# A block's products with the values issued after the next block's scores, modulation's transposes as a step of their own, and three plain pairs in the gated feed-forward

## Chip, cores, metric

One core of a Trainium2 chip. The metric is the device time of one execution in microseconds (us), smaller is better; the time of a kernel is the median of its runs.

## What is computed

Two layers of a diffusion-transformer block over 1024 latent tokens and, in layer 0, 256 context tokens beside them (1280 in all), width 1024, all in float32. Cut to what matters here:

```python
for layer in range(DEPTH):                                    # DEPTH = 2
    mod = silu(c) @ w_ada[layer] + b_ada[layer]               # modulation: shifts, scales, gates
    u = modulate(rmsnorm(x, g), sh1, sc1) @ w_in[layer]       # in-projection
    gla = gla_output(gla_chunked(q, k, v, g_fwd) + flip(gla_chunked(flip(q, k, v, g_bwd))), r)
    x = x + g1 * (concat([gla, short_conv, neighbourhood_attention]) @ w_out[layer])
    h = modulate(rmsnorm(x, norm_ffn_g[layer]), sh2, sc2)
    x = x + g2 * conv_ffn(h, w_up, conv_w, conv_b, w_down)    # dwconv3(h @ w_up), silu(a) * b, @ w_down

# gla_chunked, chunks of 16 tokens, decays b = cumsum(g):
a = where(causal, einsum(q * exp(b), k * exp(-b)), 0)         # scores inside a chunk
o = einsum(a, v) + einsum(q * exp(b), s)                      # values, and the carried state
s = s * exp(b_last) + einsum(k * exp(b_last - b), v)
```

## The kernel before, in words

Every product of the large projections is made of three TensorE matmuls on halves of the float32 numbers (`mm3`, L146 to L148: high by high, low by high, high by low). A layer runs in stages: modulation and norm, the in-projection, the gated linear attention (GLA), the neighbourhood attention (NA), `w_out`, then the feed-forward's up and down products. A scheduler sets one order for each engine when the program is built, and each engine then runs its list strictly in that order. The profile's names: PE is TensorE, DVE VectorE, ACT ScalarE, POOL GpSimd, SP the queue that issues most DMAs.

**GLA.** `gla_pair` is called for three pairs of heads. Its first loop goes over five blocks of 256 tokens: decayed keys, two transposes (L549), a copy by ACT (L551), the state products (L555). A scan by DVE (L571) then carries the state over all chunks. Its second loop goes over the output blocks, five in layer 0 and four in layer 1, so 27 in all. One block is: POOL copies the states it needs to `g_sw` (L585, L588); DVE builds the decayed queries `zq` in four operations (L601), the keys `g_k`, the masked decays `g_m` (L611) and `g_qd` (L614); PE makes the scores (L627, L635, L642) in PSUM; DVE copies the causal part to `zd` (L645), ACT copies the rest to `g_at` (L650), and DVE and POOL add into `g_at` (L653); then PE multiplies the state (L658) and the values (L662) into one PSUM bank; ACT takes the result and its square (L667, L669), PE averages the squares (L672), a gating chain follows and a DMA stores the block (L684). `zq`, `g_k` and `g_sw` have one buffer each.

PE has little of its own to do there. So `fill(cols)` draws dense in-projection matmuls from a list of generators: 1024 columns' worth after the state loop's steps, 1536 (`FO`) ahead of the scores, ahead of the values and ahead of the averages. `gla_gates` prepares the next pair's decays, also between the blocks (its products are L495). `run_background(1)`, once for each token block of the dense products, runs one step of the next layer's or stage's modulation: `ada_steps` (L158 to L194) makes four 256-column products (L176) and an addition by DVE (L181) in each of eight steps, and in the eighth, right behind that addition, two transposes by PE (L185) and the additions that store them (L189).

**Up.** PSUM has eight banks. In the up stage `up_plain` first makes `NP0` pairs of column tiles with plain products: `uc` (context tokens, one bank, layer 0 only) and `u` (1024 latent tokens, two banks for a tile). Meanwhile DVE and ACT, in `sums_b`, make the operands of a seven-product Strassen scheme, with which `ffn_up` makes the other pairs (`sx`, `sy`, L1098 to L1100) in other PSUM pools. DVE's convolution over each column tile is L1029.

Of the kernel before, what the change touches and what calls it, by code (L numbers as in the profile page):

```python
# [28 lines left out]
TB_END = [(256, 512), (768, 256), (1024, 256)]  # L29
HN = NLAT // 2  # L30
HK = KD // 2
NP0 = 2
L0, L1 = slice(NCTX, NCTX + HN), slice(NCTX + HN, T)


# [30 lines left out]
def kernel_body(ctx, tc, A, n_layers=2):  # L66
# [91 lines left out]
    def ada_steps(l, j0, nj, bufs=2):  # L158

        gw = nj * 32  # L160
        acc, st = [], {}

        def load(k):
            st[k] = ada_pool[0].tile([P, 4 * gw], F32, tag="ada_w", name="ada_w", bufs=bufs)
            SY.dma_start(out=st[k], in_=A["w_ada"][l, k * P:(k + 1) * P, j0 * P:(j0 + nj) * P])

        def step(k):
            if k == 0:
                acc.append(ada_pool[0].tile([P, gw], F32, tag="ada", name="ada"))
# [12 lines left out]
            if k == KD - 1:  # L182
                pt = dbank() if "d" in PS else bank()
                for s in range(nj // 4):
                    PE.transpose(pt[:, s * P:(s + 1) * P], acc[0][:, s * P:(s + 1) * P], ident)  # L185
                mo = mod[l][:, j0:j0 + nj, :].rearrange("p (g s) v -> p s g v", g=4)
                bi = prm[l][:, PB_ADA + j0:PB_ADA + j0 + nj].rearrange("p (g s) -> p s g", g=4)
                for s in range(nj // 4):
                    V.tensor_tensor(  # L189
                        out=mo[:, s],  # L190
                        in0=pt[:, s * P:(s + 1) * P].rearrange("p (g v) -> p g v", g=4)[:, :, 0:2],
                        in1=bi[:, s][:, :, None].to_broadcast([P, 4, 2]), op=ALU.add)

        return [lambda k=k: step(k) for k in range(KD)]  # L194

    def ada_chain(l, j0s, nj):

# [187 lines left out]
    def gla_proj(l, pA, pB, tbs_q):  # L385
# [35 lines left out]
            in_proj(l, ct, TB_ALL if (i > 0 or l < n_layers - 1) else TB_LAT, ev_qk)  # L421


        w = pA.tile([P, KD * 32], F32, tag="g_wglr", name="g_wglr")
        SY.dma_start(out=w, in_=A["wglr"][l])
        ps = dbank()
        for k in range(KD):
# [21 lines left out]
                if gates[1]:  # L449
                    gates[1].pop(0)()  # L450
        zq = pA.tile([P, 2, 4, P], F32, tag="zq", name="zq")
        zd = [pA.tile([P, 2, 4, 32], F32, tag=f"zd{i}", name=f"zd{i}") for i in range(2)]

        St = pA.tile([P, P, NT], F32, tag="g_St", name="g_St")
        G.memset(St, 0.0)
        for z in (zq, *zd):
            G.memset(z, 0.0)
        return gates[0], (glr, cst, vtok, St, (zq, zd))

# [53 lines left out]

        return (Pc, Rf, Ds), [lambda g=g, t0=t0, n=n: group(g, t0, n) for g, (t0, n) in enumerate(TG)] + [decays]

    def gla_pair(l, p, pA, glr, cst, vtok, St, zz, tbs, gates, ahead):

        zmask = cst["zmask"]
        zq0, zd = zz
# [17 lines left out]
        for t0 in range(0, T, SB):  # L537
            n, ti, nt = SB, t0 // P, SB // P
            kk = load2("g_k", kt, kr, t0, n)
            e = w256("g_e0", 2)  # L540
            G.tensor_tensor(out=e.rearrange("p (t c) -> p t c", c=P),
                            in0=Rf[:, ti:ti + nt, 0:1].to_broadcast([P, nt, P]),
                            in1=P3[:, ti:ti + nt, :], op=ALU.subtract)
            S.activation(out=e, in_=e, func=AF.Exp, scale=IT)
            V.tensor_tensor(out=e, in0=e, in1=kk, op=ALU.mult)
            fill(FS)
            pt = bank(n)
            for s in range(nt):
                PE.transpose(pt[:, s * P:(s + 1) * P], e[:, s * P:(s + 1) * P], ident)  # L549
            ket = w256("g_ket", 2)  # L550
            S.activation(out=ket, in_=pt, func=AF.Copy)  # L551
            fill(FS)
            u = bank(n)
            for s in range(nt):
                PE.matmul(u[:, s * P:(s + 1) * P], ket[:, s * P:(s + 1) * P],  # L555
                          vtok[:, ti + s, p * P:(p + 1) * P], start=True, stop=True)


            u3 = u.rearrange("p (t c) -> p c t", c=P)
            nf = min(nt, NT - 1 - ti)  # L560
# [12 lines left out]
        for t0 in range(tbs[0][0], T, SB):  # L573
# [7 lines left out]
            mm = pA.tile([P, 2, SB], F32, tag="g_m", name="g_m", bufs=2)  # L581
            SY.dma_start(out=mm, in_=md[l][p, :, :, t0:t0 + n])
            Pb = Pc[:, t0:t0 + n]
            sw = w256("g_sw")
            G.tensor_copy(out=r3(sw)[0:64], in_=St[0:64, :, ti:ti + nt].rearrange("p c s -> p s c"))  # L585
            for j in range(nt):
                sb = (1 if ti < 2 else 11) - ti - j
# [21 lines left out]
            S.activation(out=ee, in_=ee, func=AF.Abs)  # L609
            S.activation(out=ee, in_=ee, func=AF.Exp, scale=IT)  # L610
            V.tensor_tensor(out=mm, in0=ee, in1=mm, op=ALU.mult)  # L611
            qd = w256("g_qd")
            S.activation(out=qd, in_=Pb, func=AF.Exp, scale=IT)
            V.tensor_tensor(out=qd, in0=qd, in1=q, op=ALU.mult)  # L614

# [28 lines left out]
            zdt = zd[ti // nt % 2]  # L644
            V.copy_predicated(zdt.rearrange("p t g c -> p t (g c)"),  # L645
                              zmask.bitcast(U32).rearrange("p g c -> p (g c)")[:, None, :].to_broadcast([P, nt, P]),
                              zp.rearrange("p (t c) -> p t c", c=P))
            at = pA.tile([P, 2, 2, P], F32, tag="g_at", name="g_at", bufs=2)
# [1 line left out]
                S.activation(out=at[:, :, h], in_=x4[h], func=AF.Copy)  # L650
            for c in range(4):
                cs = slice(32 * c, 32 * c + 32)
                (V if c < 2 else G).tensor_tensor(out=at[cs, :, :, cs], in0=zdt[cs, :, 0:2], in1=zdt[cs, :, 2:4], op=ALU.add)  # L653
            fill(FO)
            op = bank(n)
            for s in range(nt):
                oc = slice(s * P, (s + 1) * P)
                PE.matmul(op[:, oc], sw[:, oc], qd[:, oc], start=(s == 0), stop=False, skip_group_check=True)  # L658
            for s in range(nt):
                oc = slice(s * P, (s + 1) * P)  # L660
                for h in range(2):
                    PE.matmul(op[64 * h:64 * h + 64, oc], vtok[:, ti + s, p * P + 64 * h:p * P + 64 * h + 64],  # L662
                              at[:, s, h, :], start=False, stop=True, skip_group_check=True)


            o_ = w256("g_o")
            S.activation(out=o_, in_=op, func=AF.Copy)  # L667
            sq = w256("g_sq")
            S.activation(out=sq, in_=op, func=AF.Square)  # L669
            fill(FO)  # L670
            ms = bank(n)
            PE.matmul(ms, bones, sq, start=True, stop=True)  # L672
            rt = w256("g_r", 2)
            SY.dma_start(out=rt, in_=rd[l][p, :, t0:t0 + n])
            m, a = log_sigmoid(pA, rt, n, None, "g_y")
            ex = w256("g_sq")
            S.activation(out=ex, in_=ms, func=AF.Ln, bias=eps_t[:, 0:1])
            V.scalar_tensor_tensor(out=ex, in0=ex, scalar=0.5, in1=a, op0=ALU.mult, op1=ALU.add)
            V.tensor_tensor(out=ex, in0=m, in1=ex, op=ALU.add)
            S.activation(out=ex, in_=ex, func=AF.Exp, scale=-1.0)  # L680
            V.scalar_tensor_tensor(out=o_, in0=o_, scalar=prm[l][:, PB_GNG:PB_GNG + 1], in1=rt,
                                   op0=ALU.mult, op1=ALU.mult)
            G.tensor_tensor(out=o_, in0=o_, in1=ex, op=ALU.mult)
            SY.dma_start(out=mixd[l][p, :, t0:t0 + n], in_=o_)  # L684
        for step in ahead:
            step()

# [662 lines left out]
    for l in range(n_layers):  # L1350
# [37 lines left out]
        open_psum(s=5)  # L1388
        for p in range(3):
            na_proj(l, p, pB)  # L1390
        for p in range(3):
            after, steps = gla_gates(l, p + 1, pA, *gp[:2]) if p < 2 else (None, [])
            gla_pair(l, p, pA, *gp, tbs, gates, steps)
            gates = after
        fill(None)
        pA.release()
        pB.release()
# [46 lines left out]
        pA.release()  # L1444

        close_psum("s", "d")
        open_psum(uc=1, u=2, s=3)
        pT = open_pool("pT", "left")
        Tt = {j: [tuple(pT.tile([P, HN], F32R, tag=f"t{j}{k}{c}", name=f"t{j}") for c in "hl") for k in range(HK)]
              for j in (2, 3, 4)}  # L1450
# [188 lines left out]
```

## Time and profile before

| | |
|---|---|
| median of 3 runs | 3089.65 us (3087.1 to 3096.79) |
| the profiled execution | 3087.57 us, of it the profile's span 3085.6 us |
| mean granted clock of TensorE | 0.972 of full speed |
| busy PE / DVE / ACT / POOL | 2903.3 / 2016.6 / 1271.5 / 227.8 us |

The profile's page gives each engine's busy time, the span in slices, the chain of work that ended last, and the costliest groups. Queries of the trace give the same for one engine, one line or one stretch. Start times are us from the span's start. An "idle before" is time in which the engine stood still, put down to what released it. The granted clock is TensorE's clock as a share of full speed, 2.4 GHz at 1.0 and 1.2 GHz near 0.5.

### The profile page before, as it was taken

How to read it: one execution, taken by the hardware profiler on the slowest of the kernel's cores; microseconds unless marked ns; L12 is line 12 of the kernel's file. 1: busy time of each engine (PE TensorE's matmuls, PEld its weight loads, DVE VectorE, ACT ScalarE, POOL GpSimd, SP SyncE). 2: the span in 40 equal slices, each digit the busy share in tenths (PEclk: the TensorE clock that was granted, in tenths of full speed). 3: DMA queues.
4: the chain of work that ended last, by engine and by line, in shares of the span. 5: the costliest groups of instructions: out<-in, count | busy, mean ns of one | idle time of the engine just before them, and what ended most of it. 6: DMA issues, size and time to landing. Idle time of an engine off the chain costs nothing.

```text
span 3085.6 us, 45198 instructions
## 1 busy us (share of the span) xinstructions
PE 2903.3 (94%) x17362; PEld 2343.6 (76%) x17362; DVE 2016.6 (65%) x3281; ACT 1271.5 (41%) x2350; POOL 227.8 (7%) x395
## 2 busy tenths in 40 slices
PE   6899899999899999989999799899998999998997
PEld 4676678888778888878888676677886788886886
DVE  6245664455866666768777536654548777777776
ACT  5155644354534444432112336644444444443212
POOL 0023331010000000000000003320000000000000
PEclk9999999999999999999999899999999999998998
DMA  6535556452122222243212335557532122224321
GB/s 227 159 93 164 170 175 181 126 140 86 50 88 87 88 88 88 74 158 138 93 59 82 101 100 158 166 176 200 160 90 96 69 82 82 82 82 170 117 82 55
DMA packets 258503, 361.02 MB, mean 117 GB/s; under 512 B 114288, under 2 KB 177136, under 8 KB 258288
## 3 DMA queue, kind: packets, MB, share of 16 engines
q1 hardware_dynamic: 258000, 356.95, 36.5%
q8 instruction: 137, 2.24, 0.3%
q0 software_dynamic: 288, 1.18, 0.1%
q14 instruction: 78, 0.64, 0.1%
HBM read 276.92 MB, written 81.13 MB: 116 GB/s over the span
## 4 chain that ended last, share of the span: by engine, by line
PE 74%; DVE 5%; ACT 2%; DMA 2%; issue 1%; POOL 1%; SPq 1%; DVEq 0%; ACTq 0%; POOLq 0%
PE sx L1098 5%; PE sx L1100 5%; PE sx L1099 5%; PE sy L1098 4%; PE sy L1099 4%; PE sy L1100 4%; PE uc L1099 1%; PE uc L1100 1%; PE uc L1098 1%; PE u L146 1%; PE u L147 1%; PE u L148 1%; DMA x<-xf 0%; DVE n_acc L266 0%; DVE wlo L142 0%
## 5 line engine op out<-in xcount | busy, mean ns | idle before, releaser
L141 ACT ACTIVATE whi<-wst 128x1024 fp32r<-128x1024 f32 (+1 forms) x112 | 112.7, 1023 | 465.6 <-DMA wst<-wdn 44.3
L142 DVE TENSOR_TENSOR wlo<-wst,whi 128x1024 fp32r<-128x1024 f32 (+1 forms) x112 | 132.3, 1184 | 96.6 <-ACT whi L141 94.5
L1012 ACT ACTIVATE whi<-wst 128x1024 fp32r<-128x1024 f32 x88 | 84.1, 958 | 114.8 <-PE uc L1099 70.7
L1013 DVE TENSOR_TENSOR wlo<-wst,whi 128x1024 fp32r<-128x1024 f32 x88 | 96.8, 1102 | 49.1 <-ACT whi L1012 49.1
L1012 ACT ACTIVATE s34h<-wst 128x1024 fp32r<-128x1024 f32 x40 | 42.4, 1061 | 166.5 <-PE sy L1099 163.0
L1108 DVE TENSOR_TENSOR ca<-sy,ca 128x512 f32<-128x512 f32 x80 | 55.3, 691 | 75.2 <-PE sy L1100 75.2
L1099 PE MATMUL uc<-hl,whi 128*128 128x256 f32 x320 | 90.6, 283 | 0.0
L1100 PE MATMUL uc<-hh,wlo 128*128 128x256 f32 x320 | 90.5, 283 | 0.0
L1098 PE MATMUL uc<-hh,whi 128*128 128x256 f32 x320 | 90.4, 282 | 0.0
L1037 POOL DMA_DIRECT2D gd<-v x2 | 1.4, 684 | 1168.0 <-DVE v L1035 1168.0
L1013 DVE TENSOR_TENSOR s12l<-s,s12h 128x1024 fp32r<-128x1024 f32 x40 | 49.0, 1225 | 45.5 <-ACT s12h L1012 45.5
L825 POOL TENSOR_SCALAR a_dg<-c_ident,a_sm 128x128 f32<-128x128 f32 x108 | 43.0, 398 | 444.1 <-DVE a_sm L821 311.8
L1104 ACT ACTIVATE ca<-sx 128x512 f32<-128x512 f32 x80 | 46.7, 584 | 60.0 <-PE sx L1100 60.0
L1098 PE MATMUL sx<-hh,whi 128*128 128x512 f32 x160 | 63.6, 398 | 6.2 <-DVE v L1029 6.2
L146 PE MATMUL u<-hh,whi 128*128 128x512 f32 x128 | 53.6, 428 | 15.4 <-ACT hh L308 9.5
L1098 PE MATMUL sx<-t,s12h 128*128 128x512 f32 x160 | 62.9, 393 | 2.5 <-ACT s12h L1012 2.5
L1034 ACT ACTIVATE v<-v 128x1280 f32<-128x1280 f32 (+1 forms) x44 | 51.4, 1169 | 33.0 <-DVE v L1029 32.9
L601 DVE TENSOR_TENSOR zq<-g_q,g_g 32x256 f32<-32x256 f32 x108 | 56.3, 521 | 13.1 <-ACT g_g L595 11.5
L1098 PE MATMUL sx<-t,s34h 128*128 128x512 f32 x160 | 64.4, 402 | 0.0
L265 ACT ACTIVATE n_sq<-x 128x512 f32<-128x512 f32 (+1 forms) x84 | 45.5, 552 | 44.6 <-DVE x L927 23.2
L1100 PE MATMUL sx<-hh,wlo 128*128 128x512 f32 x160 | 63.6, 397 | 0.0
L1099 PE MATMUL sx<-hl,whi 128*128 128x512 f32 x160 | 63.3, 396 | 0.0
(8035 smaller groups left out, 9892.3 us busy)
## 6 DMA issues: line engine op xcount, KB each, us to landing
wst<-wup SPq DMA_DIRECT2D x88, 512.0 KB, 3.4
ada_w<-w_ada SPq DMA_DIRECT2D x80, 512.0 KB, 4.1
wst<-win SPq DMA_DIRECT2D x48, 512.0 KB, 4.3
wst<-wdn SPq DMA_DIRECT2D x44, 512.0 KB, 3.6
f_v<-gd SPq DMA_DIRECT2D x22, 640.0 KB, 4.3
a_q<-nq SPq DMA_DIRECT2D x108, 128.0 KB, 3.7
gd<-v SPq DMA_DIRECT2D x21, 640.0 KB, 2.9
f_v<-gd SPq DMA_DIRECT2D x22, 512.0 KB, 4.2
```

Source lines behind the costliest of these rows:

```text
L141: S.activation(out=hi, in_=st, func=AF.Copy)
L142: V.tensor_tensor(out=lo, in0=st, in1=hi.bitcast(F32), op=ALU.subtract)
L146: PE.matmul(ps, whi, hhi, start=first, stop=False)
L601: V.tensor_tensor(out=zq0[r, :, g, :], in0=r3(q)[r], in1=r3(g0)[r], op=ALU.mult)
L1012: S.activation(out=hi, in_=src, func=AF.Copy)
L1013: V.tensor_tensor(out=lo, in0=src, in1=hi.bitcast(F32), op=ALU.subtract)
L1034: last_silu[0] = S.activation(out=a, in_=a, func=AF.Silu)
L1098: PE.matmul(ps, hi[:, c], bh, start=first and k == 0, stop=False, skip_group_check=True)
L1099: PE.matmul(ps, hi[:, c], bl, start=False, stop=False, skip_group_check=True)
L1100: PE.matmul(ps, lo[:, c], bh, start=False, stop=k == len(ks) - 1, skip_group_check=True)
L1104: S.activation(out=out, in_=ps, func=AF.Copy)
L1108: V.tensor_tensor(out=out, in0=ps, in1=sb, op=ALU.add)
```

## The change

It has three parts. (1) Of an output block in `gla_pair`, everything from the state product to the store becomes a function `finish`, which is put on a list `late` and called later: after the next block's scores, masks and additions and one `fill(FO)`; the last block of a pair after the next pair's first transposes; the very last after one more `fill(FO)`. `g_sw` and `g_qd` get two buffers, `zd` has one where it had two, and `g_wglr` shares the memory of a decay tile. (2) Modulation's transposes and their additions become a ninth step, so that they run one background step behind the eighth product and its addition. (3) `NP0` is 3 where it was 2, so three pairs of each layer are plain products and one fewer goes by the Strassen scheme, and the up stage's PSUM is split `uc=1, u=3, s=1` where it was `uc=1, u=2, s=3` (a `u` has two banks, the others one).

```diff
-NP0 = 2
+NP0 = 3
...
@@ ada_steps
-            if k == KD - 1:
-                pt = dbank() if "d" in PS else bank()
-                for s in range(nj // 4):
-                    PE.transpose(pt[:, s * P:(s + 1) * P], acc[0][:, s * P:(s + 1) * P], ident)
...
-        return [lambda k=k: step(k) for k in range(KD)]
+
+        def turn():
+            pt = dbank() if "d" in PS else bank()
+            for s in range(nj // 4):
+                PE.transpose(pt[:, s * P:(s + 1) * P], acc[0][:, s * P:(s + 1) * P], ident)
...
+        return [lambda k=k: step(k) for k in range(KD)] + [turn]
...
-        w = pA.tile([P, KD * 32], F32, tag="g_wglr", name="g_wglr")
+        w = pA.tile([P, T], F32, tag="g_D0", name="g_wglr")[:, :KD * 32]
...
-        zd = [pA.tile([P, 2, 4, 32], F32, tag=f"zd{i}", name=f"zd{i}") for i in range(2)]
+        zd = pA.tile([P, 2, 4, 32], F32, tag="zd", name="zd")
...
@@ gla_pair(..., late)
                 PE.transpose(pt[:, s * P:(s + 1) * P], e[:, s * P:(s + 1) * P], ident)
+            if late:
+                late.pop(0)()
             ket = w256("g_ket", 2)
...
-            sw = w256("g_sw")
+            sw = w256("g_sw", 2)
...
-            qd = w256("g_qd")
+            qd = w256("g_qd", 2)
...
             fill(FO)
-            op = bank(n)
...
+            if late:
+                late.pop(0)()
+
+            def finish(t0=t0, n=n, ti=ti, nt=nt, sw=sw, qd=qd, at=at):
+                op = bank(n)
...
+            late.append(finish)
...
+        late = []
         for p in range(3):
             after, steps = gla_gates(l, p + 1, pA, *gp[:2]) if p < 2 else (None, [])
-            gla_pair(l, p, pA, *gp, tbs, gates, steps)
+            gla_pair(l, p, pA, *gp, tbs, gates, steps, late)
             gates = after
+        fill(FO)
+        late.pop(0)()
         fill(None)
...
-        open_psum(uc=1, u=2, s=3)
+        open_psum(uc=1, u=3, s=1)
```

PE's order in layer 0, second pair of heads, first block: L627 are the scores, L658 and L662 the state and value products, `db__` dense products, L176 modulation, L672 the averages. Before:

```order
L148 MATMUL db__2849<-hh_148,wlo 128x512
L627 MATMUL sb__2913<-zq,g_k_2878 32x128 x8
...
L148 MATMUL db__2849<-hh_157,wlo 128x512
L658 MATMUL sb__2965<-g_qd,g_sw 128x128 x2
L662 MATMUL sb__2965<-g_at,vtok 64x128 x4
L146 MATMUL db__2849<-hh_160,whi 128x512
...
L176 MATMUL db__2992<-ada_w,cT 32x256 x4
...
L672 MATMUL sb__3005<-g_sq,c_bones 128x256
L495 MATMUL sb__3055<-glr,gc_wg 128x384
...
L627 MATMUL sb__3075<-zq,g_k_3040 32x128 x8
```

The same place in the changed kernel, whose lines are L631 for the scores, L665 and L669 for the products, L679 for the averages and L496 for the gates:

```order
L631 MATMUL sb__2903<-zq,g_k_2868 32x128 x8
...
L148 MATMUL db__2839<-hh_157,wlo 128x512
L496 MATMUL sb__2987<-glr,gc_wg 128x384
...
L176 MATMUL db__3014<-ada_w,cT 32x256 x4
...
L148 MATMUL db__3020<-hh_142,wlo 128x512
L631 MATMUL sb__3027<-zq,g_k_2972 32x128 x8
...
L148 MATMUL db__3020<-hh_151,wlo 128x512
L665 MATMUL sb__3079<-g_qd,g_sw 128x128 x2
L669 MATMUL sb__3079<-g_at,vtok 64x128 x4
...
L679 MATMUL sb__3110<-g_sq,c_bones 128x256
```

The products of block 1 have moved behind the scores of block 2 and nine more dense matmuls, and between the scores of blocks 1 and 2 stand 18 dense matmuls (9, 3 and 6), a gate product and a modulation step. DVE's list at this place has kept its order: before, the scan over the state, the next pair's gate decays (L497 to L499), the mask copy of block 1, then the keys and `zq` of block 2 around the additions into `g_at`:

```order
L571 SCALAR_TENSOR_TENSOR g_St<-g_D_2644,g_St 128x1280
L497 TENSOR_TENSOR g_ym<-g_ym,g_ya 128x384
L498 SCALAR_TENSOR_TENSOR g_P<-gc_smask,g_ym 64x384
L499 SCALAR_TENSOR_TENSOR g_P<-gc_smask,g_ym 64x384
L645 COPY_PREDICATED zd_1522<-gc_zmask,sb__2913 128x256
L598 TENSOR_TENSOR g_k_3040<-g_e_3035,g_k 128x256
L601 TENSOR_TENSOR zq<-g_q,g_g_3037 32x2x128 x2
L653 TENSOR_TENSOR g_at<-zd_1522 32x4x32 x2
L601 TENSOR_TENSOR zq<-g_q,g_g_3037 32x2x128 x2
```

and in the changed kernel:

```order
L575 SCALAR_TENSOR_TENSOR g_St<-g_D_2578,g_St 128x1280
L498 TENSOR_TENSOR g_ym<-g_ym,g_ya 128x384
L499 SCALAR_TENSOR_TENSOR g_P<-gc_smask,g_ym 64x384
L500 SCALAR_TENSOR_TENSOR g_P<-gc_smask,g_ym 64x384
L648 COPY_PREDICATED zd<-gc_zmask,sb__2903 128x256
L602 TENSOR_TENSOR g_k_2972<-g_e_2967,g_k 128x256
L605 TENSOR_TENSOR zq<-g_q,g_g_2969 32x2x128
L656 TENSOR_TENSOR g_at<-zd 32x4x32 x2
L605 TENSOR_TENSOR zq<-g_q,g_g_2969 32x2x128 x3
```

Only one `zq` operation has changed sides there; what has moved is PE's list against it. In the up stage of layer 0, PE's list went from the second plain tile straight to the context product of the third:

```order
L148 MATMUL u_8386<-hh7_5974,wlo_8144 128x512
L146 MATMUL uc_8560<-hh0_5960,whi_8549 128x256
...
L146 MATMUL u_8561<-hh0_5960,whi_8549 128x512
```

and the changed kernel starts the third tile's latent product, 17 matmuls of it, ahead of the context product:

```order
L146 MATMUL u_8559<-hh0_5958,whi_8547 128x512
...
L147 MATMUL u_8559<-hl5_5969,whi_8547 128x512
L146 MATMUL uc_8558<-hh0_5958,whi_8547 128x256
```

## Rows read from the trace of the kernel before

**Rows 1.** Page, part 1: busy us (share of span) x instructions, by engine

```profile
PE 2903.3 (94%) x17362; PEld 2343.6 (76%) x17362; DVE 2016.6 (65%) x3281; ACT 1271.5 (41%) x2350; POOL 227.8 (7%) x395
```

**Rows 2.** Windows, both GLA stages: length; PE, PEld, DVE, ACT, POOL busy; clock; DMA; GB/s

```profile
199.50:466.00 266.50, 244.84 (x2273) 180.27 (x2272) 164.54 (x338) 149.44 (x378) 92.32 (x142) 0.96 0.56 168
1848.00:2071.00 223.00, 202.98 (x1829) 147.55 (x1828) 139.50 (x285) 130.32 (x327) 76.17 (x115) 0.97 0.55 168
```

**Rows 3.** Line L662 on PE: what ended PE's idle time before it; us, times

```profile
  DVE g_at L653: 15.7, 9
  POOL g_at L653: 7.5, 5
  ACT g_ym L474: 4.4, 3
  ACT g_qd L613: 2.4, 1
```

**Rows 4.** Timeline, PE, layer 0, second pair: start, us, engine, line, operation

```profile
307.62 0.64 PE L176 MATMUL db__2843<-ada_w,cT 128*32 128x256 f32 x8
...
309.53 0.91 PE L495 MATMUL sb__2893<-glr,gc_wg 32*128 32x384 f32 x2
...
312.61 0.65 PE L627 MATMUL sb__2913<-zq,g_k 128*32 128x128 f32 x16
...
313.96 0.50 PE L146 MATMUL db__2849<-hh,whi 128*128 128x512 f32 x1
...
319.64 0.66 PE L662 MATMUL sb__2965<-g_at,vtok 128*64 128x128 f32 x8 [2.25 <-DVE g_at L653]
...
323.20 0.63 PE L148 MATMUL db__2998<-hh,wlo 128*128 128x512 f32 x1
323.62 0.63 PE L146 MATMUL db__2998<-hh,whi 128*128 128x512 f32 x1
```

**Rows 5.** Windows: a stretch of the up stage with nothing but 512-column matmuls

```profile
2600.00:2650.00 50.00, 50.00 (x222) 41.40 (x221) 39.49 (x43) 25.28 (x30) 0.00 (x0) 1.00 0.23 80
```

**Rows 6.** Windows: twelve stretches at the lower clock; first, last and their sum

```profile
228.80:232.30 3.50, 3.50 (x10) 2.81 (x9) 2.66 (x5) 1.82 (x6) 2.52 (x4) 0.51 0.61 185
...
2386.00:2392.90 6.90, 5.84 (x14) 4.61 (x15) 6.90 (x10) 3.79 (x4) 0.00 (x0) 0.51 0.29 115
sum 52.20, PE 48.01 PEld 37.97 DVE 38.37 ACT 25.94 POOL 11.43; mean PE 4.00 PEld 3.16 DVE 3.20 ACT 2.16 POOL 0.95
```

**Rows 7.** Line L185 on PE: what ended PE's idle time before it; us, times

```profile
  DVE ada L181: 6.2, 4
```

**Rows 8.** Timeline, DVE and PE, layer 0 second pair, layer 1 last pair, first blocks

```profile
311.00 2.83 DVE L571 TENSOR_TENSOR_SCAN g_St<-g_D,g_St 128x1280 f32<-128x1280 f32 x1 [1.04 <-ACT g_St L568]
...
314.31 1.30 DVE L498 TENSOR_TENSOR_SCAN g_P<-gc_smask,g_ym 64x384 f32<-64x384 f32 x1
...
318.54 0.95 DVE L653 TENSOR_TENSOR g_at<-zd 32x128 f32<-32x128 f32 x2
319.52 1.35 DVE L601 TENSOR_TENSOR zq<-g_q,g_g 32x256 f32<-32x256 f32 x2
...
2022.75 0.52 PE L627 MATMUL sb__18348<-zq,g_k 128*32 128x128 f32 x9
...
2026.52 2.55 DVE L601 TENSOR_TENSOR zq<-g_q,g_g 32x256 f32<-32x256 f32 x4
```

**Rows 9.** Line L601: count, ns min/median/max, first and last start, form

```profile
L601 DVE TENSOR_TENSOR zq<-g_q,g_g x108: 403/422/840, 212.5 to 2051.2; 32x256 f32<-32x256 f32 x108
```

**Rows 10.** Waits of PE, whole span: us in total, times, longest us

```profile
PE sx L1098 <- DVE v L1029: 6.2, 2, 4.3
...
PE u L146 <- DVE v L1029: 5.4, 1, 5.4
PE uc L146 <- DVE v L1029: 3.6, 1, 3.6
```

**Rows 11.** Windows, up stage of layer 1, plain products to first Strassen products

```profile
2344.00:2416.00 72.00, 54.62 (x204) 40.17 (x203) 64.86 (x89) 38.22 (x52) 0.00 (x0) 0.91 0.14 51
```

More of the change, by code (lines that the diff above doesn't have):

```diff
@@ L181, in step @@
                 V.tensor_tensor(out=acc[0], in0=ps[:, :gw], in1=acc[0], op=ALU.add)
-            if k == KD - 1:
-                pt = dbank() if "d" in PS else bank()
-                for s in range(nj // 4):
-                    PE.transpose(pt[:, s * P:(s + 1) * P], acc[0][:, s * P:(s + 1) * P], ident)
[L186 to L192, printed above, removed]
-        return [lambda k=k: step(k) for k in range(KD)]
+        def turn():
+            pt = dbank() if "d" in PS else bank()
+            for s in range(nj // 4):
+                PE.transpose(pt[:, s * P:(s + 1) * P], acc[0][:, s * P:(s + 1) * P], ident)
+            mo = mod[l][:, j0:j0 + nj, :].rearrange("p (g s) v -> p s g v", g=4)
+            bi = prm[l][:, PB_ADA + j0:PB_ADA + j0 + nj].rearrange("p (g s) -> p s g", g=4)
+            for s in range(nj // 4):
+                V.tensor_tensor(
+                    out=mo[:, s],
+                    in0=pt[:, s * P:(s + 1) * P].rearrange("p (g v) -> p g v", g=4)[:, :, 0:2],
+                    in1=bi[:, s][:, :, None].to_broadcast([P, 4, 2]), op=ALU.add)
+        return [lambda k=k: step(k) for k in range(KD)] + [turn]
     def ada_chain(l, j0s, nj):
@@ L451, in gla_proj @@
         zq = pA.tile([P, 2, 4, P], F32, tag="zq", name="zq")
-        zd = [pA.tile([P, 2, 4, 32], F32, tag=f"zd{i}", name=f"zd{i}") for i in range(2)]
+        zd = pA.tile([P, 2, 4, 32], F32, tag="zd", name="zd")
         St = pA.tile([P, P, NT], F32, tag="g_St", name="g_St")
         G.memset(St, 0.0)
-        for z in (zq, *zd):
+        for z in (zq, zd):
             G.memset(z, 0.0)
@@ L514, in gla_gates, with gla_pair @@
         return (Pc, Rf, Ds), [lambda g=g, t0=t0, n=n: group(g, t0, n) for g, (t0, n) in enumerate(TG)] + [decays]
-    def gla_pair(l, p, pA, glr, cst, vtok, St, zz, tbs, gates, ahead):
+    def gla_pair(l, p, pA, glr, cst, vtok, St, zz, tbs, gates, ahead, late):
         zmask = cst["zmask"]
@@ L643, in gla_pair @@
                                   mm[r, 1, s * P + o:s * P + o + 64], start=True, stop=True)
-            zdt = zd[ti // nt % 2]
-            V.copy_predicated(zdt.rearrange("p t g c -> p t (g c)"),
+            V.copy_predicated(zd.rearrange("p t g c -> p t (g c)"),
                               zmask.bitcast(U32).rearrange("p g c -> p (g c)")[:, None, :].to_broadcast([P, nt, P]),
@@ L652, in gla_pair @@
                 cs = slice(32 * c, 32 * c + 32)
-                (V if c < 2 else G).tensor_tensor(out=at[cs, :, :, cs], in0=zdt[cs, :, 0:2], in1=zdt[cs, :, 2:4], op=ALU.add)
+                (V if c < 2 else G).tensor_tensor(out=at[cs, :, :, cs], in0=zd[cs, :, 0:2], in1=zd[cs, :, 2:4], op=ALU.add)
             fill(FO)
-            op = bank(n)
-            for s in range(nt):
-                oc = slice(s * P, (s + 1) * P)
-                PE.matmul(op[:, oc], sw[:, oc], qd[:, oc], start=(s == 0), stop=False, skip_group_check=True)
@@ L659, in gla_pair @@
[L659 to L684, printed above, removed]
+            if late:
+                late.pop(0)()
+            def finish(t0=t0, n=n, ti=ti, nt=nt, sw=sw, qd=qd, at=at):
+                op = bank(n)
+                for s in range(nt):
+                    oc = slice(s * P, (s + 1) * P)
+                    PE.matmul(op[:, oc], sw[:, oc], qd[:, oc], start=(s == 0), stop=False, skip_group_check=True)
+                for s in range(nt):
+                    oc = slice(s * P, (s + 1) * P)
+                    for h in range(2):
+                        PE.matmul(op[64 * h:64 * h + 64, oc], vtok[:, ti + s, p * P + 64 * h:p * P + 64 * h + 64],
+                                  at[:, s, h, :], start=False, stop=True, skip_group_check=True)
+                o_ = w256("g_o")
+                S.activation(out=o_, in_=op, func=AF.Copy)
+                sq = w256("g_sq")
+                S.activation(out=sq, in_=op, func=AF.Square)
+                fill(FO)
+                ms = bank(n)
+                PE.matmul(ms, bones, sq, start=True, stop=True)
+                rt = w256("g_r", 2)
+                SY.dma_start(out=rt, in_=rd[l][p, :, t0:t0 + n])
+                m, a = log_sigmoid(pA, rt, n, None, "g_y")
+                ex = w256("g_sq")
+                S.activation(out=ex, in_=ms, func=AF.Ln, bias=eps_t[:, 0:1])
+                V.scalar_tensor_tensor(out=ex, in0=ex, scalar=0.5, in1=a, op0=ALU.mult, op1=ALU.add)
+                V.tensor_tensor(out=ex, in0=m, in1=ex, op=ALU.add)
+                S.activation(out=ex, in_=ex, func=AF.Exp, scale=-1.0)
+                V.scalar_tensor_tensor(out=o_, in0=o_, scalar=prm[l][:, PB_GNG:PB_GNG + 1], in1=rt,
+                                       op0=ALU.mult, op1=ALU.mult)
+                G.tensor_tensor(out=o_, in0=o_, in1=ex, op=ALU.mult)
+                SY.dma_start(out=mixd[l][p, :, t0:t0 + n], in_=o_)
@@ L1390, in kernel_body @@
             na_proj(l, p, pB)
+        late = []
         for p in range(3):
             after, steps = gla_gates(l, p + 1, pA, *gp[:2]) if p < 2 else (None, [])
-            gla_pair(l, p, pA, *gp, tbs, gates, steps)
+            gla_pair(l, p, pA, *gp, tbs, gates, steps, late)
             gates = after
+        fill(FO)
+        late.pop(0)()
         fill(None)
```

## Prediction

> **What bounds the kernel now.** I read the page's busy times first: PE works for 2903.3 us of the 3085.6 [rows 1], no other engine for more than two thirds of it. So the time is PE's list, its idle time, and the stretches in which its clock is down. Next the windows of the two GLA stages: in each PE is idle for about 20 us (266.50 − 244.84 = 21.7, 223.00 − 202.98 = 20.0) while DVE is busy for 62% of the time [rows 2], so no other engine is full there; PE must be waiting for single results. The view of the line of the values says which: it stood idle for 15.7 + 7.5 us until the additions into `g_at`, 4.4 and 2.4 until ACT, 30.0 us in 18 waits (over 27 blocks) [rows 3]. One of them in order of time: nine dense matmuls from 313.96 cover the way from the scores to the masked scores, and then PE waits 2.25 us for DVE [rows 4].
>
> The wait costs more than itself. Behind it two dense matmuls start 0.42 us apart [rows 4], while 222 of them in 50 us, 0.225 each, is the rate at full clock [rows 5]. In these stretches the windows show a granted clock of 0.51, the 1.2 GHz level. I found twelve of them that begin after an idle stretch which the change touches: seven after waits for the values (27.2 us of PE's busy time), three after waits for modulation's transposes (9.5), two at waits in the up stage (11.4); together 48.01 us busy [rows 6]. At 0.42 against 0.225, 47% of that is lost.
>
> **The change, part by part,** against the profiled execution's own 3087.57 us.
>
> *Values behind the next scores.* In the new order the values of block 1 stand behind 18 dense matmuls, the scores of block 2 and nine more dense matmuls; what they need, the additions, DVE ends at 318.54 + 0.95 = 319.49 [rows 8], and with the second scores no earlier than 320.87 (below), 1.35 us of them and 9 × 0.225 of dense work, PE would ask for it at 324.2, 4.8 us later. All 30.0 us go, and 27.2 × 0.47 = 12.8 us of lower clock: **−42.8**.
>
> What is late next: `zq` of block 2. Between the scores of blocks 1 and 2 PE now has 1.35 us of scores (312.61 to 313.96), 18 × 0.225 = 4.05 of dense work, a gate product (0.91) and a modulation step (0.64) [rows 4, 5], 6.95 in all. DVE's list has there the scan over the state, 2.83 us, the scans of the gates, 1.30 for the first, and the additions, and its last `zq` ends at 319.52 + 1.35 = 320.87 [rows 8], 8.26 us after the scores began. So PE will wait some 1.3 us for it. By the same reckoning the four first blocks not shown give 1.7 to 2.6, and the last pair of layer 1, whose list has no gate product, 2026.52 + 2.55 − 2022.75 = 6.32 [rows 8] less 6.04, 0.3. The six make 10.5. It happens at second blocks alone, since later ones have again a values product, the averages and their filling ahead of the scores and no scan on DVE. I let three of the six, those of about 2 us and more, pull the clock down for one stretch of 3.5 us (the length of the stretch at 228.80 [rows 6]): 3 × 3.5 × 0.47 = 4.9. **+15.4**. For waits that I can't see in this trace, at the state copy behind a deferred block above all, the bounds are nothing and, if each of the six pair starts had one of about 2 us like the 2.25 seen [rows 4], 13; I take 3, near the lower end because a filling of 1024 columns stays between that copy and its reader. **+3.0**.
>
> Costed at nothing: the second buffers of `g_sw` and `g_qd` are what lets the order stand; the single `zd` is written a block after its readers, which the DVE list shows; the shared `g_wglr` is read long before the decays come. If one of these covers were gone, a write would wait behind PE, which is how the slower rival below begins.
>
> *Transposes one step later.* The 6.2 us of waits for DVE's last addition [rows 7] go, since a token block's dense products now lie between. Of the clock, 9.5 × 0.47 = 4.5. The transposes and additions themselves remain; four steps a layer fall into the NA stage now, the same work elsewhere. **−10.7**.
>
> *Up stage.* With three `u` slots (six banks, and `uc` one, `s` one) the third tile's products have a bank pair at once: the wait for L1029 ahead of `u` in layer 1 (5.4) goes, and in layer 0 17 matmuls (3.8 us) run ahead of the context product, which covers its 3.6 [rows 10]. With both, the clock's 11.4 × 0.47 = 5.4. The waits of `sx` for the convolution, 6.2 in all [rows 10], stay: its banks still come from the last plain pair. A plain pair has 96 latent matmuls of 512 columns, a Strassen pair 84; one more in each layer is 24 × 0.225 = **+5.4**. Sum: −3.6 − 5.4 − 5.4 + 5.4 = **−9.0**. Its doubt: DVE is busy there for 64.86 of 72 us [rows 11], so a wait removed can come back as a longer wait of `sx`; against that, the extra pair gives DVE 21.6 us of PE work to catch up. The ends are −14.4 and 5.4 slower.
>
> Sum: −42.8 + 15.4 + 3.0 − 10.7 − 9.0 = −44.1, so 3043.5 against 3087.57. The median shown is 2.1 above the profiled execution, so on the runs' footing **3045**.
>
> **Rivals.**
>
> *More comes back at the pair starts (0.20).* POOL now makes two blocks' state copies right behind the scan, while DVE builds `zq` of block 2. `zq` has taken 403 to 840 ns, 422 in the middle [rows 9]: the same operation, same shape, at times doubled. If the seven operations in the chain to the second scores each took 420 ns more, 2.9 us would be added at each of six pair starts, 17.6, and the three waits that had not pulled the clock down would: 4.9. 3045 + 22 = 3067. For it speaks that range of durations; against it that the middle is at the low end. The Trainium skill, "SBUF — State Buffer", section "Who interferes with whom", says that a VectorE instruction with two SBUF inputs contends with a GpSimd instruction that reads SBUF, and that whoever holds the shared ports keeps them for its whole instruction. By that rule the two would meet at every pair start and the time would be this rival's 3067; the trace agrees as far as the 840 ns go, while most of the 108 operations took half of that.
>
> *The second blocks don't wait (0.15).* If DVE gets to `zq` earlier, because PE's values and the gating chain no longer stand between its operations, 10.5 + 4.9 + 3 = 18 us of the sum don't come: 3027.
>
> *The up stage gives nothing (0.06).* The waits move to `sx` whole and the extra products are paid: −9.0 becomes +5.4: 3045 + 14 = 3059. The full DVE speaks for it [rows 11].
>
> *Slower (0.04).* The scores of all 27 blocks starve. `zq` and `g_k` have one buffer each, so DVE can begin a block's `zq` only when PE has done the scores before; with the values out of the way, that time between scores shrinks and the wait stands at every block where it stood at 18. It becomes slower than before by over 0.3% from 3099 − 3045 = 54 us, 2.0 us at each of 27 blocks, the size of the 2.25 us wait removed [rows 4]. Against it: the middle blocks keep their work, values and averages included, between two scores, and PE's whole list per block does not shrink.
>
> **The numbers.** 0.55 for the forecast, 0.20, 0.15, 0.06 and 0.04 for the rivals. The likeliest case by itself spans 3035 to 3055 (the small waits at 0 or at 13, the clock after second-block waits in none or in all six). The range for eight in ten takes in the first two rivals: **3027 to 3068**. A measurement of this kernel tells about 0.3%, 9.3 us, from no change. Faster by more than that means under 3080: all of the forecast and the second and third rivals, and of the first all but a quarter, 0.05, where the pair starts give back over 35 us: 0.91. Within 0.3% 0.05, slower 0.04.
>
> **What would show it.** Right: no idle time to speak of ahead of the values; at second blocks PE's first score product waits 1 to 3 us for `zq`, six times; nothing ahead of modulation's transposes; the waits of `u` and `uc` for L1029 gone, those of `sx` there; PE's busy time lower by about 22 us in lower-clock stretches and higher by the 24 matmuls; the two GLA windows shorter by some 35 us together. Wrong: `zq` at 600 ns and more beside POOL's copies; score products waiting in later blocks; idle time ahead of the values as before; waits of `sx` above 12 us.

## The result, and the profile after

The changed kernel takes 3068.21 us, the median of four runs (3063.28 to 3071.19), against 3089.27 for the kernel before (four runs): a ratio of 0.9926 with an interval of 0.9905 to 0.9947. It is 21 us faster, half of what was forecast, and stands at the upper end of the range, 3068: the median lies 0.2 us above it, and by the ratio on the 3089.65 of the prediction's time it would be 3066.8. The profiled executions stand 3087.57 to 3069.08, 18.5 us apart, with spans of 3085.6 and 3067.3.

The page's busy times, after (answers to [rows 1]):

```profile
PE 2900.8 (95%) x17386; PEld 2337.9 (76%) x17386; DVE 2005.8 (65%) x3263; ACT 1260.1 (41%) x2338; POOL 229.0 (7%) x393
```

PE has 24 matmuls more, as the third plain pairs make it, and is still busy for all but 5% of the span. Where the 18.3 us of span came from is read by comparing the starts of the same work in both traces:

| start of | before, us | after, us | gained since the row above |
|---|---|---|---|
| first scores of layer 0 | 220.9 | 222.1 | −1.2 |
| eighth pair of NA score products | 505.7 | 511.1 | −4.2 |
| first feed-forward norm | 750.1 | 755.5 | 0 |
| last context product, layer 0 | 1362.1 | 1359.7 | 7.8 |
| first scores of layer 1 | 1869.6 | 1866.5 | 0.7 |
| feed-forward norm of layer 1 | 2334.5 | 2321.1 | 10.3 |
| last Strassen product | 2798.0 | 2777.4 | 7.2 |
| end | 3085.6 | 3067.3 | −2.3 |

So the two up stages gave 15 us, the attention of layer 1 gave 10, and the attention of layer 0, where the change moves most, took 4. The windows of the second and the sixth row, before (columns as in [rows 2]):

```profile
220.90:505.70 284.80, 263.45 (x2433) 197.16 (x2432) 176.60 (x391) 154.99 (x402) 93.49 (x150) 0.96 0.60 175
1869.50:2334.50 465.00, 441.58 (x3500) 343.78 (x3499) 262.44 (x625) 227.19 (x591) 91.46 (x157) 0.99 0.54 158
```

and after (the second begins 0.5 us ahead of the first scores):

```profile
222.10:511.10 289.00, 262.98 (x2432) 194.44 (x2431) 175.69 (x390) 153.16 (x401) 94.31 (x150) 0.96 0.58 172
1866.00:2321.10 455.10, 439.15 (x3502) 342.35 (x3500) 264.91 (x624) 225.12 (x591) 92.14 (x157) 0.99 0.55 161
```

PE's idle time is 21.4 before and 26.0 after in layer 0, 23.4 and 16.0 in layer 1. It has not gone, it stands elsewhere. The line of the values, L669, has no idle time ahead of it any more, and neither have the transposes, L186; the 30.0 and 6.2 us of [rows 3, 7] are gone. The view of the line of the averages, L679, after:

```profile
  ACT g_sq L676: 26.6, 14
```

and of the first score product, L631:

```profile
  DVE zq L605: 8.0, 5
```

The scores wait for `zq` at second blocks as forecast. The averages wait for ACT's squares of the values, 26.6 us in 14 waits; the same view before, of L672:

```profile
  ACT g_sq L669: 1.0, 2
```

Here is the longest, in layer 0, second pair, at the place of [rows 4]. PE in the timeline, after:

```profile
321.55 0.66 PE L669 MATMUL sb__3079<-g_at,vtok 128*64 128x128 f32 x8
...
324.09 0.39 PE L148 MATMUL db__3020<-hh,wlo 128*128 128x512 f32 x1
328.53 1.22 PE L679 MATMUL sb__3110<-g_sq,c_bones 128*128 128x256 f32 x2 [4.05 <-ACT g_sq L676]
```

DVE's last operations for `zq` in the same stretch:

```profile
325.70 1.78 DVE L605 TENSOR_TENSOR zq<-g_q,g_g 32x256 f32<-32x256 f32 x3
```

and ACT:

```profile
324.19 0.40 ACT L617 ACTIVATE g_qd<-g_P 128x256 f32<-128x256 f32 x1
327.51 0.42 ACT L599 ACTIVATE g_g<-g_e 128x256 f32<-128x256 f32 x1 [2.92 <-DVE zq L605]
327.84 0.37 ACT L674 ACTIVATE g_o<-sb__3079 128x256 f32<-128x256 f32 x1
328.10 0.38 ACT L676 ACTIVATE g_sq<-sb__3079 128x256 f32<-128x256 f32 x1
```

The values were done at 322.2, and nothing kept ACT from squaring them but its own list: the exponential `g_g` (L599) for a later block stands ahead, and it waits for DVE to have read its one buffer for `zq`, until 327.48. The copy and the square come behind it. The two views of that exponential, before (L595, on ACT):

```profile
  DVE zq L601: 28.0, 18
```

and after (L599):

```profile
  DVE zq L605: 41.5, 18
```

ACT had stood there before too. At this place its list had the exponential of block 3 ahead of the square of block 1, released when the second `zq` was read, at 320.87 [rows 8], about when the values were done, 319.64 + 0.66 = 320.30 [rows 4]. Now it is the exponential of block 4 that stands ahead of that square, and it is released by the third `zq`.

The waits of PE after that answer to [rows 10], and two that are new:

```profile
PE sx L1107 <- ACT s12h L1021: 5.0, 2, 2.5
...
PE sb__4872 L783 <- DMA a_q<-nq: 3.0, 1, 3.0
...
PE sb__4760 L783 <- DVE a_nm L806: 1.7, 1, 1.7
```

Those of `u`, `uc` and `sx` for the convolution are gone altogether. The last two are at the start of the NA stage of layer 0, where PE had no idle time before. Those 25 us, before and after:

```profile
465.00:490.00 25.00, 25.00 (x169) 20.58 (x168) 12.60 (x40) 12.46 (x39) 2.97 (x8) 1.00 0.76 178
```

```profile
465.00:490.00 25.00, 20.13 (x124) 15.70 (x122) 9.33 (x31) 9.41 (x30) 2.25 (x6) 0.86 0.80 204
```

After, 4.9 us are idle, and a stretch at the lower clock (475 to 482, 5.21 us of it busy) takes some 2.4 us more (47% of 5.21). PE came to this place with some 17 more dense matmuls done than before (the last product of the first short-convolution tile started at 470.01, and at 475.12 before), and waited there.

### The profile page after: what moved, and what is told of

Same layout as the page of the kernel before. It is cut to its first block, busy times and chain, and to the rows that moved or that the text cites. A ratio compares the mean times of both kernels' runs of the same rounds, so it can differ in the third digit from the quotient of the medians.

```text
span 3067.3 us, 45224 instructions
## 1 busy us (share of the span) xinstructions
PE 2900.8 (95%) x17386; PEld 2337.9 (76%) x17386; DVE 2005.8 (65%) x3263; ACT 1260.1 (41%) x2338; POOL 229.0 (7%) x393
## 5 line engine op out<-in xcount | busy, mean ns | idle before, releaser
L146 PE MATMUL u<-hh,whi 128*128 128x512 f32 x192 | 76.6, 405 | 10.0 <-ACT hh L309 9.5
L148 PE MATMUL u<-hh,wlo 128*128 128x512 f32 x192 | 76.8, 402 | 0.7 <-DVE wlo L1022 0.7
L147 PE MATMUL u<-hl,whi 128*128 128x512 f32 x192 | 76.4, 400 | 0.5 <-DVE hl L310 0.5
L605 DVE TENSOR_TENSOR zq<-g_q,g_g 32x256 f32<-32x256 f32 x108 | 57.2, 529 | 13.0 <-ACT g_g L599 11.6
L1244 ACT ACTIVATE hh<-f_v 128x1280 fp32r<-128x1280 f32 (+1 forms) x36 | 41.0, 1159 | 50.3 <-DMA f_v<-gd 50.3
```

The lines of the kernel that those rows point to most:

```text
L146: PE.matmul(ps, whi, hhi, start=first, stop=False)
L147: PE.matmul(ps, whi, hlo, start=False, stop=False)
L148: PE.matmul(ps, wlo, hhi, start=False, stop=last)
L605: V.tensor_tensor(out=zq0[r, :, g, :], in0=r3(q)[r], in1=r3(g0)[r], op=ALU.mult)
```

## The experiments

Ratios are to the kernel before, measured on the same chip beside each run.

**The parts alone.** e1 keeps only the deferral:

```diff
-NP0 = 3
+NP0 = 2
...
-        return [lambda k=k: step(k) for k in range(KD)] + [turn]
+        return [lambda k=k: step(k) for k in range(KD)]
...
-        open_psum(uc=1, u=3, s=1)
+        open_psum(uc=1, u=2, s=3)
```

> Deferred values alone, without the ninth modulation step and with two plain pairs and the old PSUM split. Theory A (the squares for the averages, made by ACT, are held back behind another operation of ACT, and that hands back what the deferral gave): idle time ahead of the averages (L679's place) some 20 to 30 us, none ahead of the values, and the time within 10 us of the kernel before, 3080 to 3095. Rival B (the deferral gives what I summed, some 24 us, and it is modulation or the up stage that failed): 3060 to 3070.

3074.24 us, ratio 0.9949 (0.9934 to 0.9964): 16 us faster, more than theory A had room for and less than rival B. The line of the averages (L678 here):

```profile
  ACT g_sq L675: 23.4, 13
```

So the hand-back belongs to the deferral itself, but it is not the whole gain.

e2, the kernel before with the ninth step alone:

```diff
-        return [lambda k=k: step(k) for k in range(KD)]
+        return [lambda k=k: step(k) for k in range(KD)] + [turn]
```

> Modulation's transposes as a ninth step alone. By the sum of the prediction 6.2 us of waits and 4.5 of lower clock go: 3079 against 3089. Rival: the wait moves to the next thing that DVE is late with, the additions into g_at: idle time ahead of the values above 30 us by as much, and the time within 4 us of before.

3085.68 us, ratio 0.9980 (0.9969 to 0.9992): 6 us. The line of the values (L663 here), against the 30.0 us of [rows 3]:

```profile
  DVE g_at L654: 24.8, 14
  POOL g_at L654: 6.8, 4
  ACT g_qd L614: 4.1, 2
  ACT g_ym L475: 3.7, 3
```

39.4 us. The rival holds for the idle time: what PE no longer waits at the transposes it waits at the values, and more. The profile's mean clock was 0.977 against 0.972; but the profiled execution (3079.80) is the second fastest of ten, whose clocks go from 0.971 to 0.977, so where the 6 us of the median lie is not shown.

e3, the kernel before with the up stage's part alone:

```diff
-NP0 = 2
+NP0 = 3
...
-        open_psum(uc=1, u=2, s=3)
+        open_psum(uc=1, u=3, s=1)
```

> Three plain pairs and the PSUM split 1, 3, 1 alone, on the kernel before. The trace of the changed kernel lets me expect about 15 us less, 3074, more than the 9 of the prediction, since the waits of sx for the convolution go too and with them two stretches of lower clock. Rival (9 as predicted, the rest of the difference being chance): 3080.

3078.33 us, ratio 0.9961 (0.9947 to 0.9974): 12 us, with an interval of 8 to 16, which holds both numbers. The line of the first Strassen products, `sx`:

```profile
  ACT s12h L1012: 5.0, 2
```

e4 has the second of those two edits alone.

> The PSUM split 1, 3, 1 alone, still two plain pairs: separates the third slot from the third pair. If the slot alone removes the waits of u and uc, idle time ahead of those is zero and sx waits longer, by 5 us or more, since DVE has no third pair's time to catch up: 3080 to 3086. If the slot needs the third pair to be of use at all: no change, 3089 within 3.

3081.18 us, ratio 0.9964 (0.9947 to 0.9982), 11 us. The same line, which makes both `sx` and `sy`:

```profile
  ACT s12h L1012: 7.7, 2
  DVE v L1029: 2.7, 1
```

The slot alone removes the waits of `u` and `uc`, and the Strassen products wait 10.4 us (`sx` 7.7, `sy` 2.7) where `sx` waited 8.7 (6.2 for the convolution and 2.5 for its operands). The third pair takes 5.4 us off that and costs 5.4 us of matmuls: by these two it pays for itself and no more. The time is in the expected band, but the wait grew by 1.7 us and not by 5 or more; the time can't be told from e3.

e8, the change without its deferral (e2 and e3 in one):

> The change without the deferral: ninth modulation step, third plain pair and PSUM split. If the deferral hands back all that it gives, this is as fast as the whole change or faster: 3060 to 3068. If the deferral is worth what I summed (24 us), this is slower than the whole change by more than 10: above 3078.

3071.69 us, ratio 0.9941 (0.9925 to 0.9958). Neither bound was met: the whole change, 0.9926, is 0.0015 better, less than the intervals tell. On top of the other two parts the deferral is worth about 5 us by the medians, which these intervals don't tell from nothing; alone it is worth 16. The windows of the NA start show where some 6 us of that are. First e8:

```profile
465.00:490.00 25.00, 23.57 (x149) 17.33 (x148) 9.60 (x32) 9.53 (x30) 2.24 (x6) 1.00 0.90 226
```

and then e1:

```profile
465.00:490.00 25.00, 24.45 (x157) 19.57 (x155) 9.24 (x31) 9.17 (x28) 2.23 (x6) 1.00 0.86 202
```

Idle 1.4 and 0.6 us, full clock. The 4.9 us and the lower clock there come only where the deferral and the ninth step are together; all seven kernels below that have both (e5, e6, e7 and e9 to e12) show 4.0 to 5.9 idle and 0.86 in this window.

**What holds the square.** All of these start from the changed kernel. e5 issues it ahead of the copy:

```diff
-                o_ = w256("g_o")
-                S.activation(out=o_, in_=op, func=AF.Copy)
                 sq = w256("g_sq")
                 S.activation(out=sq, in_=op, func=AF.Square)
+                o_ = w256("g_o")
+                S.activation(out=o_, in_=op, func=AF.Copy)
```

> The changed kernel with ACT's square of the values issued ahead of their copy, so that the square does not stand behind the copy's wait for the store of the block before. Theory A1 (at pair ends the copy waits for the one g_o buffer's store and holds the square): the waits of about 3 us ahead of the averages at pair ends go, 10 us of the 26.6 and two or three stretches of lower clock, 3055. Rival A2 (all of it is the exponential of a later block that stands ahead, waiting for zq): no change, 3068 within 4.

3061.35 us, ratio 0.9909 (0.9894 to 0.9924): not told from the changed kernel by time. The line of the averages:

```profile
  ACT g_sq L674: 19.0, 13
```

7.6 us less. In the changed kernel ACT's copy waited 12.8 us, in five waits, for the store of the block before out of the one `g_o` buffer, with the square behind it. Of A1 only a part holds: at the four pair ends 7.5 of 10.4 us are left. At three of these ends, and at the very last block, the square now waits on ACT for POOL's multiplication of the block before, which reads the one `g_sq` buffer:

```profile
  POOL g_o L690: 2.0, 4
```

e6 gives the exponential three buffers:

```diff
-            g0 = w256("g_g0")
+            g0 = w256("g_g0") if ti // nt % 3 == 0 else w256("g_ket", 2)
```

> The changed kernel with three buffers in place of one for the exponential that zq reads (the other two are those of the state loop's keys, free at that time). Theory A2 (that exponential waits for VectorE's reads of its one buffer and stands ahead of the square on ACT): ACT's 41.5 us of waits ahead of it shrink to under 20, the waits ahead of the averages in the middle blocks (4.1, 2.3, 1.5, 2.5 us and others, about 12 us) shrink to under 5, and the time is 3055 to 3062. Rival A1 (pair ends and the store alone): no change, 3068 within 4.

3065.32 us, ratio 0.9918 (0.9904 to 0.9933): not told from the changed kernel by time. The line of the averages, and then that of the exponential on ACT:

```profile
  ACT g_sq L676: 20.3, 14
```

```profile
  POOL g_e L596: 34.6, 12
```

The waits for `zq` are gone from the exponential, all 41.5 us, and in their place it waits 34.6 us for its own operand from POOL. With more buffers the scheduler put it further ahead in ACT's list, so it is early by one more block and waits for the next single thing. A2's size was wrong for that reason.

e7 has both edits.

> Both edits in one. If A1 and A2 each hold for its share, nearly all of the 26.6 us ahead of the averages goes, with its stretches of lower clock: 3040 to 3050, and idle time ahead of the averages under 6 us. If the square is late for a third reason, it stays above 15 us.

3056.29 us, ratio 0.9894 (0.9878 to 0.9910), the lowest median here, 10 us under the changed kernel by the ratios. But the averages still wait:

```profile
  ACT g_sq L674: 17.8, 13
```

The third reason is of the same kind: some other ACT operation stands ahead of the square. So e9 tests the order itself. It makes the exponential depend on the square of two blocks before:

```diff
                 S.activation(out=sq, in_=op, func=AF.Square)
+                S.activation(out=zb, in_=sq[:, 0:1], func=AF.Copy, scale=0.0)
...
-            S.activation(out=g0, in_=e0, func=AF.Exp, scale=IT)
+            S.activation(out=g0, in_=e0, func=AF.Exp, scale=IT, bias=zb[:, 0:1])
```

> The changed kernel with the exponential for zq made dependent on the square of two blocks before (its bias is a zero that ACT makes out of that square), so that ACT can no longer have it ahead of that square. If ACT's order is the cause of the late squares in the middle blocks: idle time ahead of the averages falls from 26.6 to 12 or less, the pair ends remaining; the scores of later blocks then wait for zq, more than the 8.0 us of now, because the exponential comes later. Time 3055 to 3070 by how these two weigh. If the square is late for another reason, the idle time ahead of the averages stays above 20.

3073.22 us, ratio 0.9945 (0.9930 to 0.9959). The averages (L682 here) and the scores (L633):

```profile
  ACT g_sq L678: 12.2, 10
```

```profile
  DVE zq L607: 20.9, 12
```

With the exponential behind the square, 14.4 us of the 26.6 go; of what is left 8.2 us are at the four pair ends, and no other wait is above 0.7. And 12.9 us come back at the scores, since `zq` is later by that much: one of the two is late whichever ACT does first.

How much of the 26.6 was the exponential can be read from ACT's timeline in the changed kernel. It stands right ahead of the square, waiting for `zq`, at three of the fourteen waits, the averages at 240.8, 328.5 and 344.1 (2.3, 4.1 and 0.7 us). All three are gone in e9, so for these 7.1 us the cause is shown. Ahead of the other squares stand other operations, each waiting for something else:

```profile
263.93 0.22 ACT L511 ACTIVATE g_Ds<-g_Rf 64x9 f32<-64x9 f32 x1 [2.38 <-DVE g_Rf L506]
...
286.80 0.38 ACT L674 ACTIVATE g_o<-sb__2605 128x256 f32<-128x256 f32 x1 [2.79 <-DMA mixd<-g_o]
...
1988.42 0.63 ACT L613 ACTIVATE g_ee<-g_ee 128x512 f32<-128x512 f32 x1 [0.89 <-POOL g_ee L611]
```

The next pair's decays (L511) are ahead at two waits of PE (2.6 us), the copy with its store (L674) at three (8.0), the decays `g_ee` (L613), which wait for POOL, at six (8.9). For these the cause is read from the order of ACT's list and not tested one by one; that they too are shorter in e9 may come from PE's asking later, since it now waits at the scores.

e10 leaves ACT's part alone and moves PE's cover:

```diff
-            fill(FO)
             if late:
-                late.pop(0)()
+                late.pop(0)(2 * FO)
+            else:
+                fill(FO)
...
-                fill(FO)
+                fill(cols)
                 ms = bank(n)
```

> The changed kernel with the dense filling of 1536 columns that stands ahead of the deferred values put behind them, so that 18 dense matmuls in place of 9 stand between values and averages. The squares are held until the same moment, the averages are asked for 2 us later: of the 26.6 us ahead of them about 5 remain (each wait less 2.0), none appears ahead of the values, whose operands were ready nearly 5 us early. 22 us and some lower clock: 3042 to 3050. Rival: values asked for earlier wait for the additions again, and the gain is half.

3075.22 us, ratio 0.9952 (0.9937 to 0.9967): no gain on the changed kernel, and 8 us slower by the ratios, though the two intervals still overlap. The waits ahead of the averages fell to 17.7 in 8, not to 5, and new ones came ahead of dense products and modulation, such as these in layer 1 (the longest new one, 4.0 us ahead of a modulation product in layer 0, is put down to nothing that the profile shows):

```profile
PE db__18599 L176 <- DVE ada L181: 1.8, 1, 1.8
PE db__17181 L146 <- DVE p_lo L759: 1.5, 1, 1.5
```

As I read it, eighteen dense matmuls in one piece ask for results of DVE that nine don't. The expectation took the moment of the square as fixed; it is not, since the whole order was made anew. e11 adds e10's edit to e7.

> The moved filling, the square ahead of the copy and the three buffers in one: idle time ahead of the averages under 3 us, 3035 to 3045. If the moved filling alone has done it, no better than it within 4 us.

3071.73 us, ratio 0.9941 (0.9925 to 0.9958), with 13.2 us ahead of the averages: some 15 us slower than e7. Missed.

e12 is e7 with a pair's last block finished one state block later:

```diff
-            if late:
+            if late and t0 > 0:
                 late.pop(0)()
             ket = w256("g_ket", 2)
```

> The kernel of e7 (square first, three buffers for the exponential), and a pair's last block finished one state block later in the next pair, since its square waits there for the multiplication of the block before (one g_sq buffer) when two blocks are finished close together. If that is what holds the square at pair ends, the four waits of 1.1 to 2.5 us there (7.7 of 17.7) go, with a stretch or two of lower clock: 3045 to 3050. If the wait is moved to the state block's transposes or products by the ACT operations that come with it: 3056 within 4.

3061.33 us, ratio 0.9910 (0.9897 to 0.9924): 1.3 us above the rival's band, and not faster than e7. The averages, and then the state products, L559:

```profile
  ACT g_sq L674: 10.9, 9
```

```profile
  ACT g_ket L555: 6.7, 4
```

6.9 us less at the one, and 6.7 in four waits at the other, where e7 has none. The wait moved to the keys' copy on ACT, as the rival's mechanism has it.

## Why the prediction was right, and where it was wrong

**The values.** Right. All 30.0 us ahead of them went.

**Second blocks.** Right in place and nearly in size: 8.0 us in five waits (1.0 to 2.5) where the sum had 10.5 in six. The rival by which POOL's state copies double `zq` did not come. The Trainium skill's rule on shared ports ("SBUF — State Buffer", "Who interferes with whom") may be at work in single operations, up to 897 ns, but their middle has not moved from [rows 9]. At the second blocks themselves, beside POOL's copies, the four operations had middles of 420, 586 and 584 ns in the three pairs of layer 0, and 480, 650 and 520 in the kernel before: slow for some already then, and not slower now. All blocks, after:

```profile
L605 DVE TENSOR_TENSOR zq<-g_q,g_g x108: 404/422/897, 213.8 to 2031.8; 32x256 f32<-32x256 f32 x108
```

**Waits that I couldn't see.** This is the step that failed. The sum took +3.0 us, with 13 as the upper bound, and looked for them at the state copy of the pair starts. Measured: +25.6 (26.6 less 1.0), ahead of the averages. The prediction asked of each PE instruction when its operands could be ready, and for the averages it let the nine dense matmuls stand, as they had covered the same square before. It did not ask what stands ahead of the square in ACT's list. A view that would have warned was there: the exponential on ACT, 28.0 us in 18 waits, an engine at 41% that nonetheless stands still in 18 of 27 blocks. Deferring the values put the square behind that place and behind others like it; e9 shows it for the exponential, 7.1 us of the 26.6.

**The clock.** It follows the waits. The lower-clock stretches of the two attention stages had 36.7 us of PE's busy time before (27.2 + 9.5, [rows 6]); after, seven windows add up to the last line here:

```profile
243.00:246.50 3.50, 3.50 (x25) 2.10 (x23) 1.00 (x3) 2.73 (x7) 0.73 (x1) 0.52 0.41 102
...
328.00:335.00 7.00, 6.47 (x27) 4.36 (x28) 4.31 (x11) 5.59 (x13) 3.20 (x4) 0.52 0.57 146
475.00:482.00 7.00, 5.21 (x22) 3.91 (x22) 2.83 (x10) 2.16 (x9) 1.50 (x4) 0.51 0.66 182
...
sum 31.50, PE 28.35 PEld 21.35 DVE 15.00 ACT 19.23 POOL 7.58; mean PE 4.05 PEld 3.05 DVE 2.14 ACT 2.75 POOL 1.08
```

One of them is behind the 4.05 us wait for the square, one at the NA start. 8.3 us less (36.7 − 28.35), at 47% 3.9 us, where the sum had 12.8 + 4.5 − 4.9 = 12.4.

**The transposes.** The wait went as said; the 10.7 was too much. Alone it is 6 us (e2), and its 6.2 us of idle time came back at the next thing that DVE is late with. A wait removed ahead of a later wait for the same engine is no gain by itself.

**Modulation's four steps moved.** They were costed at nothing. With the deferral they go with a loss of 7 us at the NA start of layer 0 (4.9 idle, 2.4 of clock), which neither part alone has. Why it takes both was not tried: whether it is the dense work used up earlier, the steps themselves or the loads beside them stays open.

**The up stage.** −9.0 in the sum, −12 alone (8 to 16). The step that was off is that the waits of `sx` stay: with the third pair DVE catches up, and of 8.7 us 5.0 are left. The extra pair's 5.4 us were right, and e4 shows that the PSUM split does the work.

Against the sum, then: 22.6 us more at the averages, 4.9 of idle time at the NA start and 8.5 of clock that did not come (the NA start's 2.4 among them) make it 36 us slower. The up stages gave 6 more (15.0 by the table of starts), the second blocks 2.5, and the state products, which had waited 3.4 us for the keys' copy and now wait 0.3, 3.1: 11.6 faster. That is 24 us; 3045 and 3068.2 are 23 apart. The state products' lines, before (L555) and after (L559):

```profile
  ACT g_ket L551: 3.4, 4
```

```profile
  ACT g_ket L555: 0.3, 1
```

Of the other rivals none came: the up stage did not come out at nothing, the second blocks did wait, and the scores of later blocks had no idle time ahead of them.

That the time still came out at the upper end of the range is luck. That end was put there for the first rival, 3067 by slower `zq` at the pair starts; the time came out like it by another way, which the prediction had bounded at 13 us, and the span of its likeliest case, 3035 to 3055, was missed.

## What to carry to other kernels

Before an operation is deferred, look at the in-order list of every engine that handles its result, and at what that engine waits for there: an engine that is busy for 41% can still hold the result for 4 us, because something of a later step stands ahead. More buffers don't settle that when a scheduler uses them to run further ahead (e6), and a forced order only chooses who is late (e9); what is left is to make the chain of DVE, ACT and PE through one buffer shorter, which no run here tried. And measure the parts of a change apart and together: here 16, 6 and 12 us made 21.

## What had not been expected of the hardware

The lower clock differs between runs of like code by several us. After the last Strassen product no edit touches anything, and the Strassen products from 2450 us on run at full clock; yet the time lost from 2450 us to the end to the lower clock (1 less the granted clock, times PE's busy time, summed over windows of 2 us) was 4.3 us in e12, 8.6 in the kernel before and 10.2 in the changed kernel. So a gain of a few us that a profile shows in the clock, as in e2, is not safely the edit's.
